# Negated score minima, one probability factor applied on ScalarE, finished heads spilled as one plane

## The chip, the cores and the metric

One NeuronCore of one Trainium2 chip runs the whole kernel. TensorE (PE) does matrix products, VectorE (DVE) and ScalarE (ACT) elementwise work, GpSimd (POOL) a small share of it, and SyncE (SP) issues the DMAs. Each engine takes its instructions in its own fixed order and waits at semaphores for the others. The metric is the device time of one execution in microseconds.

## The reference

A layer of two groups of eight heads over 512 tokens and 16 meta tokens, with one input projection and one output projection:

```python
u = rms_norm(h, g_norm)
rq, rk, rv, rgate, dq, dk, dv, dgate = split(u @ w_in)
r = retention(rq, rk, rv)                     # chunkwise, 8 heads of 128
r = head_layer_norm(r, g_ret) * silu(rgate)
# diff attention, per head, per block of 128 queries:
s = where(allowed, q @ k.T * scale - slope * dist, -inf)     # two maps c = 0, 1
p = softmax(s)
a = p[:, :, 0] - lam * p[:, :, 1]
d = a @ v
d = head_rms_norm(d, g_diff) * (1 - lam_init) * silu(dgate)
y = concatenate([r, d]) @ w_out
out = rms_norm(h + y, final_norm_g)
```

All of it is in float32. The kernel makes each float32 product from parts: an operand is cast to a rounded high part on ScalarE and its low part is a subtraction on VectorE.

## The kernel before

**Stages.** Up to about 130 us the first head is projected; then a loop runs over 29 column pairs of the input projection (rv/rk, rq/rg, dv/dk, dq/dg of the heads in turn), some 98 us for a head of each kind; from about 820 us the output projection runs in five column chunks. Each pair is seven products named P3, P7, P1, P6, P2, P5, P4 of 24 matmuls (`product`, L813, outputs p3, v, x, y). Their weight tiles come by DMA as four raw blocks b11, b12, b21, b22. For each product ScalarE casts the block (wh, L785) and VectorE subtracts (wl, L796); two block sums are made on VectorE (L799, L801), two on GpSimd (L803, L804, each reading two 128x1024 SBUF tiles), L804 after wl_P1 has read b11.

**Order.** `run_pair` issues these products and calls `step()` between them, which moves generators on: `diff_task` (scores, softmax, transposes, the product with the values) and `ret_task`, then `finish` for the head's norm. A scheduler of the tile framework then orders the instructions on every engine with a cost model of its own, so the written order is not what stands on an engine.

**Scores.** In `diff_task` a block b of 128 queries has two maps s. The matmuls L590 (L596 for b = 3) write the scores to one of three PSUM banks shared with other work; L604 on VectorE adds the distance bias, writes p to SBUF, and reduces the maximum mx (the reduction is a second, small instruction). L606 scales mx by -slope; L607 on ScalarE is exp(slope * p + mx) and accumulates the sums zz. L613 and L614 make the two factors rr, L615 scales the second map by rr[1], L616 adds rr[0] times the first. L629 on TensorE transposes the result (at_d), from which L633 and L634 make high and low parts; tile 0 goes through p_std (L438 to L440).

**Finished heads.** `finish` squares and sums a head's output, gets the column sums on TensorE (ms, L463), copies them to SBUF (L464), sends them by DMA to 128 partitions (mc, L467), takes the power on GpSimd (L469 to L472), sends them to DRAM and back as a broadcast (rd, L474; bc, L476, into the sq tile), multiplies (L479, L480), and casts (L485) and subtracts (L486) to the two parts that the output projection reads. Fourteen of the sixteen heads finish before the mix tiles exist; both parts go to DRAM from the r2k buffers (L490) and come back after the loop, straight into the mix tiles, by 28 DMAs of 256 KB. Retention head 7 and diff head 7 finish in output chunk 0, where `mms` runs over pairs of heads and the weight pieces pass through five wr buffers.

## Time and profile before

| | us |
|---|---|
| three runs | 1031.91, 1031.96, 1035.21 |
| median | 1031.96 |
| the profiled execution | 1036.45 |
| its span | 1034.4 |
| TensorE busy in the span | 964.7 |
| VectorE | 824.0 |
| ScalarE | 538.7 |
| GpSimd | 242.7 |

The profiled execution is 4.5 us longer than the median. The span runs from the first to the last recorded instruction. A timeline row is the start, the duration, engine, line, operation, tiles (output <- inputs) and, in brackets, how long the engine had been idle and what it waited for. The recorded durations of consecutive VectorE instructions overlap by about 0.08 us. Tile names in the trace leave out head and block numbers; the order of instructions, shown in the next section, has them.

### The profile page before, as it was taken

Reading aid. Unit: us, or ns where it says so; the run is one execution under the profiler, and the core shown is the slowest. Engines: PE = TensorE matmul, PEld = TensorE weight load, DVE = VectorE, ACT = ScalarE, POOL = GpSimd, SP = SyncE. Lnnn points to the kernel's source line nnn. Section 1 sums busy time; section 2 is a strip of 40 time slices with the busy share of each in tenths; the row PEclk is TensorE's granted clock in tenths of the full one; section 3 lists DMA queues with packets and bytes.
Section 4 is the critical chain, followed back from the end, with each engine's and each line's share of the span. In section 5 each row is a group of like instructions: output and inputs, shape, how many; then the busy total and the mean of one; then the engine's idle time right before and its main releaser. Section 6 shows DMA issues by size and latency. Waiting matters only on the chain.

```text
span 1034.4 us, 18382 instructions
## 1 busy us (share of the span) xinstructions
PE 964.7 (93%) x7215; PEld 921.6 (89%) x7215; DVE 824.0 (80%) x1332; ACT 538.7 (52%) x979; POOL 242.7 (23%) x169
## 2 busy tenths in 40 slices
PE   6999988999999999899999999999994999799997
PEld 6999988999999999899999999999983988588896
DVE  6698869899989998999899989989996754334432
ACT  6454565565656564646565656565654443223322
POOL 4453131132233213321332133233220200000001
PEclk8999999999999999999999999999997999999998
DMA  9512533353235334543643264226443496143304
GB/s 269 158 43 73 125 93 103 82 155 114 82 97 152 107 109 116 139 121 87 140 134 98 82 156 113 83 82 156 113 113 102 161 385 212 50 126 96 122 1 163
DMA packets 166405, 127.03 MB, mean 123 GB/s; under 512 B 9712, under 2 KB 145008, under 8 KB 165808
## 3 DMA queue, kind: packets, MB, share of 16 engines
q1 hardware_dynamic: 165744, 124.04, 42.2%
q10 hardware_dynamic: 576, 1.84, 0.5%
q8 instruction: 56, 0.92, 0.4%
q14 instruction: 29, 0.24, 0.1%
HBM read 107.77 MB, written 11.57 MB: 115 GB/s over the span
## 4 chain that ended last, share of the span: by engine, by line
PE 54%; DVE 21%; DMA 9%; issue 6%; POOL 6%; ACT 4%; SPq 0%; POOLq 0%; DVEq 0%; ACTq 0%
PE y L526 6%; PE y L527 5%; PE y L528 5%; DVE wl_P L796 5%; PE y_rqrg L813 4%; PE x_dvdk L813 3%; PE x_dqdg L813 3%; DMA mc_r<-sq_r 2%; PE x_rqrg L813 2%; PE y_dvdk L813 2%; PE v_rqrg L813 2%; DMA sq_r<-rd_r 2%; PE v_dvdk L813 2%; DVE p_d L615 2%; PE y_rvrk L813 2%
## 5 line engine op out<-in xcount | busy, mean ns | idle before, releaser
L785 ACT CAST wh_P<-b 128x1024 fp32r<-128x1024 f32 x203 | 212.7, 1049 | 147.9 <-DVE mx_d L606 30.3
L796 DVE TENSOR_TENSOR wl_P<-b,wh_P 128x1024 fp32r<-128x1024 f32 x203 | 260.3, 1284 | 13.0 <-ACT wh_P L785 11.0
L803 POOL TENSOR_TENSOR b<-b,b 128x1024 f32<-128x1024 f32 x29 | 69.9, 2412 | 406.1 <-DVE b L799 301.7
L104 DVE TENSOR_TENSOR wl<-wr,wh 128x1024 fp32r<-128x1024 f32 (+1 forms) x40 | 49.8, 1252 | 69.3 <-ACT wh L103 69.2
L804 POOL TENSOR_TENSOR b<-b,b 128x1024 f32<-128x1024 f32 x29 | 76.8, 2649 | 105.5 <-DVE wl_P L796 32.5
L103 ACT CAST wh<-wr 128x1024 fp32r<-128x1024 f32 (+1 forms) x40 | 40.8, 1029 | 88.7 <-PE y L528 70.1
L607 ACT ACTIVATE p_d<-p_d,mx_d 128x144 f32<-128x144 f32 (+3 forms) x64 | 36.6, 572 | 31.7 <-DVE mx_d L606 31.1
L799 DVE TENSOR_TENSOR b<-b,b 128x1024 f32<-128x1024 f32 x29 | 35.5, 1223 | 0.6
L629 PE MATMUL at_d<-ident,p_d 128*128 128x128 f32 (+1 forms) x112 | 23.1, 275 | 13.3 <-DVE p_d L616 12.9
L801 DVE TENSOR_TENSOR b<-b,b 128x1024 f32<-128x1024 f32 x29 | 35.2, 1214 | 0.1
L813 PE MATMUL x_dqdg<-uah,wh_P 128*128 128x256 f32 x128 | 32.2, 290 | 3.0 <-ACT s_dqdg L825 3.0
L1049 POOL TENSOR_SCALAR rs<-ssq,pre 128x1 f32<-128x1 f32 x4 | 1.9, 486 | 136.1 <-ACT jk L1007 136.1
L813 PE MATMUL x_dqdg<-ual,wh_P 128*128 128x256 f32 x128 | 31.2, 282 | 0.0
L526 PE MATMUL y<-wh,mix_s3h 128*128 128x512 f32 (+1 forms) x64 | 23.6, 382 | 6.3 <-ACT mix_s3h L485 5.1
L813 PE MATMUL x_dvdk<-uah,wh_P 128*128 128x264 f32 x112 | 28.5, 284 | 0.0
L813 PE MATMUL x_dvdk<-ual,wh_P 128*128 128x264 f32 x112 | 28.4, 284 | 0.0
L813 PE MATMUL x_rvrk<-uah,wh_P 128*128 128x264 f32 x112 | 28.4, 285 | 0.0
L813 PE MATMUL x_rvrk<-ual,wh_P 128*128 128x264 f32 x112 | 28.2, 285 | 0.0
L629 PEld LDWEIGHTS at_d<-ident,p_d 128*128 128x128 f32 (+1 forms) x112 | 12.8, 126 | 17.3 <-DVE p_d L616 14.8
L813 PEld LDWEIGHTS x_dqdg<-uah,wh_P 128*128 128x128 f32 x128 | 24.1, 188 | 4.2 <-ACT s_dqdg L825 4.2
L526 PE MATMUL y<-wh,mix_s2h 128*128 128x512 f32 (+1 forms) x80 | 27.8, 348 | 0.0
L528 PE MATMUL y<-wh,mix_al 128*128 128x512 f32 (+1 forms) x80 | 27.8, 348 | 0.0
(567 smaller groups left out, 3550.5 us busy)
## 6 DMA issues: line engine op xcount, KB each, us to landing
b<-in_w_in_dram SPq DMA_DIRECT2D x116, 512.0 KB, 4.6
wr<-in_w_out_dram SPq DMA_DIRECT2D x32, 512.0 KB, 4.1
kbuf<-kbuf SPq DMA_DIRECT2D x24, 264.0 KB, 4.9
wr<-in_w_in_dram SPq DMA_DIRECT2D x12, 512.0 KB, 8.5
tab<-in_decay_tab_dram SPq DMA_DIRECT2D x8, 288.0 KB, 4.3
sq_r<-rd_r SPq DMA_DIRECT2D x8, 256.0 KB, 3.6
sq_d<-rd_d SPq DMA_DIRECT2D x8, 256.0 KB, 4.2
mx<-mxh_r SPq DMA_DIRECT2D x7, 256.0 KB, 3.7
```

The costliest lines, as they stand in the source:

```text
L103: act.copy(out=hi, in_=raw)
L104: eng.tensor_tensor(out=lo, in0=raw, in1=f(hi), op=ALU.subtract)
L526: pe.matmul(o, ah, bh, start=start, stop=False)
L527: pe.matmul(o, ah, bl, start=False, stop=False)
L528: pe.matmul(o, al, bh, start=False, stop=stop)
L607: act.activation(p, p, AF.Exp, bias=mx, scale=slope, accum_out=zz[:, s:s + 1])
L629: pe.transpose(at[:n, b * P - q0:(b + 1) * P - q0], aa[b][:, kc:kc + n], ident)
L785: act.copy(out=hi, in_=raw_w[n][SOURCE[pn]])
L796: vec.tensor_tensor(out=lo, in0=w[SOURCE[pn]], in1=f(hi), op=ALU.subtract)
L803: pool.tensor_tensor(out=w["b12"], in0=w["b12"], in1=w["b11"], op=ALU.subtract)
L804: pool.tensor_tensor(out=w["b11"], in0=w["b21"], in1=w["b22"], op=ALU.subtract)
L813: pe.matmul(o, w_[:, kt, :], u[lo][:, kt, c0:], start=not add and w_ is wh and kt == 0 and lo == 0, stop=w_ is wl and kt == 7, skip_group_ ...
```

## The change

Three edits. In the scores the reduction is now a minimum of -slope times the sum (L604's successor L600), so that mx is at once the bias of the exponential, whose scale becomes -1; the 64 L606 go. The second map's factor is applied by ScalarE (L610, an ACTIVATE Copy with a per-partition scale, in place) where VectorE's L615 did it. And a finished head that has no mix tile yet goes to DRAM as it is, from its s2k buffer: 14 writes and 14 reads of 256 KB in place of 28 and 28, no cast and no subtraction in the loop. After the loop `fetch` loads them in pairs into wr buffers and splits each head into its mix tiles with a cast on ScalarE and a subtraction on VectorE, the first two pairs at once, and one more at each step of chunk 0.

```diff
-            hi, lo = heads_mix[col]
+            split(oc, *heads_mix[col])
         else:
-            hi, lo = (ap.tile([P, SEQ], F32R, tag="r2k", bufs=4, name=f"mx{t}_{nm}") for t in "hl")
-        act.copy(out=hi, in_=oc)
-        vec.tensor_tensor(out=lo, in0=oc, in1=f(hi), op=ALU.subtract)
-        if col not in heads_mix:
-            spilled[col] = dr.tile([P, 2, SEQ], F32, tag=f"mx{col}", bufs=1, name=f"mx{col}")
-            for j, t in enumerate((hi, lo)):
-                nc.sync.dma_start(out=spilled[col][:, j, :], in_=f(t))
+            spilled[col] = dr.tile([P, SEQ], F32, tag=f"mx{col}", bufs=1, name=f"mx{col}")
+            nc.sync.dma_start(out=spilled[col], in_=oc)
...
-                vec.tensor_tensor_reduce(shape(p), shape(dist[:, 384 - P * b:]), sp, op0=ALU.add, op1=ALU.max,
-                                         scale=1.0, scalar=-3e38, accum_out=mx)
-                vec.tensor_scalar(mx, mx, -slope, None, op0=ALU.mult)
-                act.activation(p, p, AF.Exp, bias=mx, scale=slope, accum_out=zz[:, s:s + 1])
+                vec.tensor_tensor_reduce(shape(p), shape(dist[:, 384 - P * b:]), sp, op0=ALU.add, op1=ALU.min,
+                                         scale=-slope, scalar=3e38, accum_out=mx)
+                act.activation(p, p, AF.Exp, bias=mx, scale=-1.0, accum_out=zz[:, s:s + 1])
...
-            vec.tensor_scalar(pp[1], pp[1], rr[:, 1:2], None, op0=ALU.mult)
+            act.activation(pp[1], pp[1], AF.Copy, scale=rr[:, 1:2])
...
-    for ks in kpairs:
-        for k in list(range(KT))[ks]:
-            if k in spilled:
-                for j, t in enumerate(heads_mix[k]):
-                    nc.sync.dma_start(out=f(t), in_=spilled[k][:, j, :])
+    fetched = set()
+    def fetch(upto):
+        for i in range(min(upto, len(kpairs))):
+            ks = [k for k in list(range(KT))[kpairs[i]] if k in spilled]
+            if i not in fetched and ks:
+                t = wp.tile([P, 1024], F32, tag="wr", bufs=5, name=f"mb{i}")
+                for j, k in enumerate(ks):
+                    nc.sync.dma_start(out=t[:, j * SEQ:j * SEQ + SEQ], in_=spilled[k])
+                for j, k in enumerate(ks):
+                    split(t[:, j * SEQ:j * SEQ + SEQ], *heads_mix[k])
+            fetched.add(i)
+    fetch(2)
...
+                    fetch(i + 3)
```

Lines below the first edit have lower numbers in the changed file: L604 is L600 there, L613, L614 and L616 are L608, L609 and L611, L518 is L513, L796 is L791, L799 and L801 are L794 and L796, GpSimd's L803 and L804 are L798 and L799, L813 is L808, L829 is L824. Over the whole program VectorE has 1238 instructions for 1334, ScalarE 927 for 895, SyncE 297 for 325, TensorE 7216 in both. TensorE's order is the same up to head 0's scores; from there the scheduler has moved work on all engines. In head 4, whose stretch is 518 to 560 us in the trace, this looks as follows.

VectorE, from the scores of block 0 to block 1's first (p_d4_1_0), before; a name is the tile with head, block and map, wl_17_P6 is the low weight part of pair 17's product P6:

```order
L604 ISA mx_d4_0_1_6540 128x1
L801 TENSOR_TENSOR b22_17_6353<-b22_17_6353,b11_17_6357 128x1024
L606 TENSOR_SCALAR mx_d4_0_0_6532<-mx_d4_0_0_6532 128x1
L693 SCALAR_TENSOR_TENSOR dq4_h_6423<-su2_dqdg4_6393,dq4_h_6423 64x256
L693 SCALAR_TENSOR_TENSOR dq4_l_6424<-su2_dqdg4_6393,dq4_l_6424 64x256
L606 TENSOR_SCALAR mx_d4_0_1_6540<-mx_d4_0_1_6540 128x1
L604 ISA p_d4_1_0_6586,mx_d4_1_0_6587<-dist_617,s_d4_1_0_6583 128x272
```

and now:

```order
L796 TENSOR_TENSOR b22_17_6281<-b22_17_6281,b11_17_6285 128x1024
...
L600 ISA p_d4_0_1_6461,mx_d4_0_1_6462<-dist_617,s_d4_0_1_6458 128x144
...
L513 TENSOR_TENSOR vbuf1_1192<-vp_d4_6439,vbuf1_1192 128x512
L688 SCALAR_TENSOR_TENSOR dq4_h_6351<-su2_dqdg4_6321,dq4_h_6351 64x256
L688 SCALAR_TENSOR_TENSOR dq4_l_6352<-su2_dqdg4_6321,dq4_l_6352 64x256
L791 TENSOR_TENSOR wl_17_P6_6526<-b22_17_6281,wh_17_P6_6524 128x1024
L600 ISA p_d4_1_0_6507,mx_d4_1_0_6508<-dist_617,s_d4_1_0_6504 128x272
```

The block sum of pair 17 (b22) has moved ahead of the scores, and between block 0 and block 1 stand a subtraction of the value split (L513) and one more weight part.

VectorE, at the same head's blocks 2 and 3, before:

```order
L614 TENSOR_TENSOR rr_d4_2_6651<-rr_d4_2_6651,neglam_619 128x1
L796 TENSOR_TENSOR wl_18_P1_6862<-b11_18_6691,wh_18_P1_6860 128x1024
...
L615 TENSOR_SCALAR p_d4_2_1_6646<-p_d4_2_1_6646,rr_d4_2_6651 128x400
L796 TENSOR_TENSOR wl_18_P6_6905<-b22_18_6687,wh_18_P6_6903 128x1024
L616 SCALAR_TENSOR_TENSOR p_d4_2_0_6638<-p_d4_2_0_6638,rr_d4_2_6651,p_d4_2_1_6646 128x400
L604 ISA p_d4_3_1_6742,mx_d4_3_1_6743<-dist_617,s_d4_3_1_6737 128x528
...
L796 TENSOR_TENSOR wl_18_P2_6935<-b21_18_6693,wh_18_P2_6933 128x1024
...
L796 TENSOR_TENSOR wl_18_P5_6985<-b12_18_6689,wh_18_P5_6983 128x1024
...
L615 TENSOR_SCALAR p_d4_3_1_6742<-p_d4_3_1_6742,rr_d4_3_6747 128x528
```

and now:

```order
L611 SCALAR_TENSOR_TENSOR p_d4_2_0_6557<-p_d4_2_0_6557,rr_d4_2_6568,p_d4_2_1_6564 128x400
L794 TENSOR_TENSOR b22_18_6604<-b22_18_6604,b12_18_6606 128x1024
L600 ISA p_d4_3_1_6658,mx_d4_3_1_6659<-dist_617,s_d4_3_1_6653 128x528
...
L791 TENSOR_TENSOR wl_18_P7_6744<-b22_18_6604,wh_18_P7_6742 128x1024
...
L796 TENSOR_TENSOR b22_18_6604<-b22_18_6604,b11_18_6608 128x1024
L609 TENSOR_TENSOR rr_d4_3_6662<-rr_d4_3_6662,neglam_619 128x1
...
L791 TENSOR_TENSOR wl_18_P1_6777<-b11_18_6608,wh_18_P1_6775 128x1024
L791 TENSOR_TENSOR wl_18_P6_6820<-b22_18_6604,wh_18_P6_6818 128x1024
L611 SCALAR_TENSOR_TENSOR p_d4_3_0_6618<-p_d4_3_0_6618,rr_d4_3_6662,p_d4_3_1_6658 128x528
L791 TENSOR_TENSOR wl_18_P2_6850<-b21_18_6610,wh_18_P2_6848 128x1024
```

Block 2's sum (L611, was L616) has moved ahead of P7's and P1's weight parts; block 3's stands behind P6's, where block 2's had stood.

TensorE, at the transposes of the same head in the product x of pair 18, before:

```order
L813 MATMUL x_rqrg5_6932<-ual_123,wh_18_P1_6860 128x256
L813 MATMUL x_rqrg5_6932<-uah_122,wl_18_P1_6862 128x256 x6
L629 MATMUL at_d4_0_6783<-ident_106,p_d4_2_0_6638 16x128
L629 MATMUL at_d4_1_6891<-ident_106,p_d4_2_0_6638 128x128
L813 MATMUL x_rqrg5_6932<-uah_122,wl_18_P1_6862 128x256 x2
```

and now:

```order
L808 MATMUL x_rqrg5_6847<-ual_123,wh_18_P1_6775 128x256
L808 MATMUL x_rqrg5_6847<-uah_122,wl_18_P1_6777 128x256 x3
L624 MATMUL at_d4_0_6698<-ident_106,p_d4_3_0_6618 16x128
L624 MATMUL at_d4_1_6806<-ident_106,p_d4_3_0_6618 128x128
L808 MATMUL x_rqrg5_6847<-uah_122,wl_18_P1_6777 128x256 x5
```

The transposes at this place take block 3 where they took block 2; those of block 2 have gone ahead of it.

ScalarE, at the end of the last diff head (7), where the last norm of the loop (diff head 6) ends, before:

```order
L607 ACTIVATE p_d7_3_0_9812,zz_d7_3_9806<-p_d7_3_0_9812,mx_d7_3_0_9813 128x528
L485 CAST mxh_d6_9906<-oc_d6_9732 128x512
L607 ACTIVATE p_d7_3_1_9863,zz_d7_3_9806<-p_d7_3_1_9863,mx_d7_3_1_9864 128x528
L877 ACT_TABLE_LOAD
L877 ACTIVATE sg_dg7_9564<-sg_dg7_9564 128x512
L825 COPY s37_rvrk7_9644<-p3_rvrk7_9645 128x264
```

and now:

```order
L602 ACTIVATE p_d7_3_1_9735,zz_d7_3_9679<-p_d7_3_1_9735,mx_d7_3_1_9736 128x528
L610 ACTIVATE p_d7_3_1_9735<-p_d7_3_1_9735,rr_d7_3_9739 128x528
L438 CAST p_std_625<-at_d7_0_9779 16x512
L439 CAST p_std_625<-at_d7_0_9779 16x512
L628 CAST ah_d7_1_9892<-at_d7_1_9887 128x512
L872 ACT_TABLE_LOAD
L872 ACTIVATE sg_dg7_9443<-sg_dg7_9443 128x512
L820 COPY s37_rvrk7_9521<-p3_rvrk7_9522 128x264
```

The cast of head 6 is gone; the Copy of block 3, two casts of transposed rows (p_std) and one of the next tile (ah) stand ahead of the table load.

TensorE, in output chunk 0, at the column sums of retention head 7 (ms_r7), whose result that chunk's last piece needs; wh19 is the high part of weight piece 19, before:

```order
L528 MATMUL y0_2_10317<-wh19_10618,mix_al_10283 128x512
L526 MATMUL y0_10314<-wh19_10618,mix_ah_10282 128x512
L527 MATMUL y0_10314<-wl19_10619,mix_ah_10282 128x512
L528 MATMUL y0_10314<-wh19_10618,mix_al_10283 128x512
L463 MATMUL ms_r7_10527<-sh_r7_10506,ones_115 128x512
L526 MATMUL y1_0_10708<-wh20_10648,mix_s4h_10276 128x512
```

and now:

```order
L522 MATMUL y0_10166<-wl18_10476,mix_ah_10148 128x512
L523 MATMUL y0_10166<-wh18_10475,mix_al_10149 128x512
L521 MATMUL y0_0_10167<-wh19_10505,mix_ah_10148 128x512
L463 MATMUL ms_r7_10407<-sh_r7_10379,ones_115 128x512
L522 MATMUL y0_0_10167<-wl19_10506,mix_ah_10148 128x512
L523 MATMUL y0_0_10167<-wh19_10505,mix_al_10149 128x512
```

The sums come before most of piece 19's matmuls, 11 matmuls earlier against the first matmul of retention head 7's own columns, which has kept its place.

## Rows read from the trace of the kernel before

**Rows 1.** The page: the span, and busy us of each engine.
```profile
span 1034.4 us, 18382 instructions
PE 964.7 (93%) x7215; PEld 921.6 (89%) x7215; DVE 824.0 (80%) x1332; ACT 538.7 (52%) x979; POOL 242.7 (23%) x169
```

**Rows 2.** Stretches: length, busy of PE, PEld, DVE, ACT, POOL; PEclk, DMA share, GB/s.
```profile
200.00:750.00 550.00, 530.18 (x4274) 520.61 (x4273) 519.95 (x826) 329.86 (x593) 156.45 (x94) 1.00 0.44 115
767.00:806.00 39.00, 23.18 (x151) 20.92 (x150) 26.46 (x64) 16.53 (x35) 4.24 (x5) 0.78 0.23 68
820.00:880.00 60.00, 60.00 (x337) 52.56 (x337) 32.94 (x51) 23.71 (x41) 4.63 (x5) 1.00 0.85 306
880.00:920.00 40.00, 33.74 (x141) 27.03 (x140) 14.11 (x17) 9.79 (x16) 1.64 (x4) 0.96 0.26 84
```

**Rows 3.** TensorE's waits from 200 to 750: total us, times, longest.
```profile
PE s_d L590 <- DVE mx_d L604: 6.7, 5, 1.4
PE at_d L629 <- DVE p_d L616: 6.7, 5, 2.0
PE x_dqdg L813 <- ACT s_dqdg L825: 3.0, 4, 1.4
```

**Rows 4.** Groups by line and form: total us, mean ns of one | idle before.
```profile
L606 DVE TENSOR_SCALAR mx_d<-mx_d 128x1 f32<-128x1 f32 x64 | 8.3, 147 | 0.2
L615 DVE TENSOR_SCALAR p_d<-p_d,rr_d 128x400 f32<-128x400 f32 x8 | 16.3, 2033 | 0.0
L607 ACT ACTIVATE p_d<-p_d,mx_d 128x400 f32<-128x400 f32 x16 | 10.0, 622 | 3.6 <-DVE mx_d L606 3.6
```

**Rows 5.** Timeline of head 4 around the wait of s_d4_2_1.
```profile
526.99 2.64 POOL L804 TENSOR_TENSOR b<-b,b 128x1024 f32<-128x1024 f32 x1
...
527.40 2.50 DVE L693 SCALAR_TENSOR_TENSOR dq_l<-su_dqdg,dq_l 64x256 fp32r<-64x256 f32 x1
...
530.01 0.43 DVE L604 CUSTOM_DVE_ANT_0 p_d<-dist,s_d 128x272 f32<-128x272 f32 x1
...
530.59 0.60 PE L590 MATMUL s_d<-kbuf,dq_l 128*128 128x400 f32 x2 [1.37 <-DVE mx_d L604]
```

**Rows 6.** Timelines of VectorE, GpSimd and TensorE in head 4, 545 to 558.
```profile
545.32 2.99 DVE L829 TENSOR_TENSOR s_rvrk<-s_rvrk,s_rvrk 128x264 f32<-128x264 f32 x2
...
551.04 1.21 DVE L796 TENSOR_TENSOR wl_P<-b,wh_P 128x1024 fp32r<-128x1024 f32 x1
...
552.87 2.56 DVE L615 TENSOR_SCALAR p_d<-p_d,rr_d 128x400 f32<-128x400 f32 x1
...
545.33 2.69 POOL L803 TENSOR_TENSOR b<-b,b 128x1024 f32<-128x1024 f32 x1 [15.71 <-DVE s_rvrk L829]
552.39 2.81 POOL L804 TENSOR_TENSOR b<-b,b 128x1024 f32<-128x1024 f32 x1 [4.37 <-issue]
...
557.16 0.39 PE L629 MATMUL at_d<-ident,p_d 128*16 128x128 f32 x2 [1.99 <-DVE p_d L616]
```

**Rows 7.** Busy time by stretch behind that wait; PEclk stands third from the end.
```profile
558.00:560.00 2.00, 2.00 (x12) 2.00 (x11) 2.00 (x3) 0.91 (x3) 0.00 (x0) 0.52 0.84 239
560.00:562.00 2.00, 2.00 (x13) 2.00 (x13) 1.68 (x5) 1.22 (x2) 0.00 (x0) 0.63 0.71 204
```

**Rows 8.** Timeline at the last diff head's end.
```profile
788.14 0.43 DVE L615 TENSOR_SCALAR p_d<-p_d,rr_d 128x400 f32<-128x400 f32 x1
...
793.61 0.69 DVE L479 TENSOR_TENSOR oc_d<-oc_d,sq_d 128x512 f32<-128x512 f32 x1 [4.37 <-DMA sq_d<-rd_d]
...
795.62 0.62 ACT L485 CAST mxh_d<-oc_d 128x512 fp32r<-128x512 f32 x1 [7.19 <-DVE oc_d L480]
...
799.23 0.59 PE L813 MATMUL y_rvrk<-s2h,wh_P 128*128 128x264 f32 x1 [9.34 <-ACT s_rvrk L825]
```

**Rows 9.** Timeline in output chunk 0: the column sums, and the wait.
```profile
882.34 0.39 PE L463 MATMUL ms_r<-sh_r,ones 128*128 128x512 f32 x1
...
896.04 0.80 PE L526 MATMUL y<-wh,mix_s3h 128*128 128x512 f32 x1 [5.13 <-ACT mix_s3h L485]
```

## The prediction

> **What bounds the kernel now.** The first view is the page's list of engines: TensorE is busy for 964.7 of 1034.4 us [rows 1], so about 70 us of the span are there to be had, and only where TensorE waits. The table by stretches says where that is: 19.8 us between 200 and 750 (the steady heads), 15.8 between 767 and 806 (the last diff head), none between 820 and 880 and 6.3 between 880 and 920 (the output projection) [rows 2]. In the steady stretch VectorE is busy for 520 of 550 us, ScalarE for 330. The list of waits then names who ends TensorE's waits: in the heads nearly always VectorE, through the score banks (s_d behind L604) and the transposes of the probabilities (at_d behind L616), 6.7 us each in five waits, and ScalarE's s_dqdg with 3.0 us [rows 3]; outside, one wait of 9.3 us and one of 5.1 us, both ended by ScalarE [rows 8, 9]. So the change can pay in three places: five or six like waits per kind in the heads, the gap before the last head's end, and the gap in output chunk 0.
>
> **Work taken off VectorE.** The 64 L606 instructions are 147 ns each, 8.3 us busy, 0.2 idle [rows 4]; less the 0.08 us by which VectorE's records overlap they hold it for 0.07 us each, so some 4 us of VectorE's own time, of which only the part ahead of a waiting TensorE counts. Of the 32 L615 the 128x400 form is 2033 ns on average over eight, 16.3 us [rows 4]. That mean is no work: at 552.87 one lasts 2.56 us because GpSimd's L804 runs from 552.39 to 555.20, and it ends 0.23 us after it [rows 6]. Beside a still GpSimd the same form takes 0.43 us [rows 8]. A removed L615 therefore returns 0.3 to 0.5 us, and the rest only if nothing else on VectorE needs the same access just then. It does: at 545.32 two L829 adds of 264 elements take 2.99 us under L803 [rows 6], and at 527.40 an L693 on 64x256 takes 2.50 us under L804 [rows 5]. Whichever instruction with two SBUF operands stands there, waits GpSimd out.
>
> The Trainium skill ("SBUF — State Buffer", "Who interferes with whom") says the same as a rule: VectorE and GpSimd share one port pair, whoever comes first holds it for the whole instruction, and an instruction with two SBUF inputs counts as one that needs it. By that rule L611 is as exposed as L615 was, and what decides is which of the two stands first at the boundary; the trace agrees for L829 (2.99 us). If VectorE's instruction were always first there, the time would be that of the first rival below.
>
> **What the scaling costs on ScalarE.** The trace of before has no such Copy. The nearest row is the Exp of L607 on the same tile, 622 ns for 400 elements [rows 4]; the Copy saves the accumulator's read and should lie at or below it. Four per head are about 2.2 us of ScalarE, which has 220 us free of 550 [rows 2]: no throughput bound. It adds two handovers, VectorE to ScalarE to VectorE, and behind a waiting Copy stand weight casts (L785) in ScalarE's order. I take 0 for three of the four blocks, since the order puts other VectorE work between L609 and L611, and 0.6 us for block 1, where L611 comes right after L609; the worst would be 0.6 for each.
>
> **The steady heads, one of them walked (head 4, 518 to 560).** Two waits matter.
>
> First, s_d4_2_1. Before, TensorE waits 1.37 us until 530.59, since L693 was held for 2.50 us by GpSimd and p_d4_1_0 comes behind it [rows 5]. Now TensorE has eight more matmuls of 0.12 us ahead of that bank (1.0 us later), but VectorE has the value split's subtraction, L513 on 512 elements (0.6 us, as the 128x512 L479 in [rows 8]) and one more wl (1.21 us, 1.14 to the next start [rows 6]) ahead of p_d4_1_0, less two L606 (0.15). Sum: 0.6 + 1.14 − 0.15 − 1.0 = +0.6; I take +0.5, the GpSimd hold being no longer than before.
>
> Second, at_d4_0, where TensorE waits 1.99 us until 557.16 for block 2's probabilities [rows 6]. By the order, the same place in TensorE's row (3063, now 3064) waits for block 3's. On VectorE block 2 has moved far ahead, no wait there any more; block 3 stands behind wl_P1 and wl_P6. When does it end? Before, wl_P1 starts at 551.04 [rows 6]. Shed ahead of it: two L615 (0.66), L486 (0.6), six L606 (0.4). Added ahead of it: L611 of block 2 and the last L600 (0.54 + 0.63), the shift of the first wait (1.5) and ScalarE's 0.6. That is 551.04 − 1.66 + 3.27 = 552.6. Then wl_P1 and wl_P6 (2 x 1.14) run to 554.9. GpSimd's L804 (L799 in the changed file) is free to start when wl_P1 has been read, waits out wl_P6, and takes the next boundary as at 545.33; 2.81 us later, at 557.7, L611 of 528 elements starts, and ends near 558.4. TensorE comes there at 555.17 + 0.5 − 0.2. So the wait would be about 2.9 us if GpSimd always wins, and 0.2 us if L611 gets in first. The five waits of before had a mean of 1.34 [rows 3]. The rows favour GpSimd (2.99 at 545.32), but the two boundaries are within a microsecond, and the heads differ a little; I take 2.0, so +0.65.
>
> Third, x_dqdg behind s_dqdg, 3.0 us in four waits [rows 3]: VectorE comes out of the head's last block earlier and the mxh casts, which stood in ScalarE's row waiting for a norm's DMA, are gone from it. I take half, −1.5 in all.
>
> Steady heads: 5 x (0.5 + 0.65) − 1.5 = +4.3 us. Bounds: −19.8 (every wait of [rows 2] gone) and +5 x (0.6 + 1.55) = +10.8.
>
> One thing makes long waits dearer: after the 1.99 us wait the granted clock is 0.52 from 558 to 560 and 0.63 from 560 to 562, that is the 1.2 GHz level for a good 3 us, about 1.7 us lost [rows 7]; over the whole stretch it is 1.00 on the mean [rows 2]. Not in the sum, but in the second rival.
>
> **The gap before the last head's end.** TensorE waits 9.34 us until 799.23 [rows 8] behind this chain: the norm's reload ends, L479 at 793.61, L480, the cast mxh_d at 795.62 (0.62), Exp, the table load, Silu, copy of s_rvrk. The cast goes. In its place ScalarE has the Copy of block 3, then two p_std casts and one ah_d cast that wait for TensorE's transposes, then the load and the Silu. From L479 on that is 0.7 + 0.8 (L611) + 0.5 (transposes) + 3 casts (1.7) + the load 1.28 + 0.63 + 0.4 = 6.0 us, against 5.6 before. But the transposes now fall into the gap (1.4 us of TensorE work that used to follow), and ms_d6 stands five TensorE rows earlier, with L450 earlier on VectorE: about 1.5 us. Sum: +0.4 − 1.4 − 1.5 = −2.5. Bounds: 0 and −4.
>
> **The output stage.** Fourteen spills of 256 KB less, each way. Writes are hidden beside the heads: 0. The reloads fall into 820 to 880, where DMA is at 0.85 of its share but TensorE never waits [rows 2]: 0, unless the new splits wait. These are 14 casts and 14 subtractions of 128x512, some 8.7 us of ScalarE and 9.7 of VectorE, in a stretch where these two have 36 and 27 us free. The later gap, 5.13 us until 896.04 [rows 9], starts from ms_r7, issued at 882.34. The same mix_s3h matmul waits, but ms_r7 stands 11 matmuls earlier (y0_0 now comes behind it): 11 x 0.226 (0.39 us each in the record [rows 9], overlapping) = 2.5 us earlier, and the chain behind it is unchanged. So −2.5; bounds 0 (the start of the chain held by ScalarE's casts in front) and −5.1.
>
> **Sum.** +4.3 − 2.5 − 2.5 and about −1.5 for head 0, whose stretch has the same instructions taken out and no walk of mine: −2.2 us. The profiled execution took 1036.45 us (its span 1034.4, 2.05 around it) and would take 1034.2; it lies 4.5 us over the median 1031.96. Put on the median: 1029.8 us. Runs of this kernel can tell apart about 0.3%, 3.1 us.
>
> **Rivals.**
> - VectorE's slack opens: L611 of block 3 gets in ahead of GpSimd in each head, at_d's 6.7 us and s_dqdg's 3.0 vanish, the first wait stays at +0.5 x 5. That is −7.2 in the heads, −6.5 elsewhere: 1018. For it: VectorE is at 520 of 550 us and loses some 4 us a head even where the long forms return only their 0.4. Against it: the order uses the room at once, by putting other work ahead of what TensorE waits for. It decides at one boundary, wl_P6 to L611.
> - The waits grow over 2 us and the clock falls with them (slower). at_d waits 2.9 us in five heads (+7.8), the first wait +2.5, and each time the clock drops once as at 558 (+1.7 x 5, one had it before, so x 4: +6.8). With −1.5 and −6.5: +9, 1041. For it: my own walk ends at 2.9, and the one wait of 1.99 had the drop. Against it: a longer wait also lets VectorE catch up for the next.
> - The splits of chunk 0 are late: ScalarE's casts wait in order for a reload behind weight pieces in the wr buffers, and TensorE, which never waits in 820 to 880, stops for one reload of some 4 us. 1034. Against it: DMA carries 3.7 MB less there.
>
> **How the numbers follow.** The forecast has 0.43, its own range being 1025 to 1035; the first rival 0.27; the second 0.22; the third 0.08. Of the forecast 0.17 lies below 1028.9, 0.23 within 0.3%, 0.03 above. The third is split among the three. So faster 0.45, same 0.27, slower 0.28. The range takes in most of both rivals: 1016 to 1041.
>
> **What would show it.** In the profile after: the 128x400 L615 rows gone, but some L611, wl or L824 rows of 2.3 us and more in their place, starting while GpSimd's L798 or L799 runs; at_d4_0 waiting on L611 of block 3, near 557; the wait before y_rvrk below 9 us with at_d matmuls inside; the wait in chunk 0 near 2.6 us. I would be wrong if GpSimd's instructions mostly met PSUM-reading VectorE work, if TensorE waits within 820 to 880, or if x_dqdg's waits grew because ScalarE is held at a Copy.

## The result and the profile after

The changed kernel takes 1049.28 us (median of 4 runs, 1048.19 to 1051.99) where the kernel before took 1032.77 beside it: a ratio of 1.016, interval 1.0133 to 1.0187. It is slower by 16.5 us; 1029.8 was forecast, with a range up to 1041. The profiled execution took 1049.42 us, its span 1047.6. The profiled execution of before lay 4.5 us over its median, so the two spans differ by 13.2 us only.

First the page's list of engines and its totals, to be read beside [rows 1]:

```profile
span 1047.6 us, 18341 instructions
...
PE 973.2 (93%) x7215; PEld 928.7 (89%) x7215; DVE 813.1 (78%) x1236; ACT 549.7 (52%) x1011; POOL 228.1 (22%) x169
...
HBM read 104.10 MB, written 7.90 MB: 107 GB/s over the span
```

VectorE has lost 10.9 us of busy time, ScalarE has gained 11.0, as meant. The span grew by 13.2 all the same. TensorE, with the same number of matmuls, is busy for 8.5 us more and idle for 4.7 more, so the time is in its clock and in its waits. The table by stretches, for [rows 2] (the columns are the stretch, then the busy time of each engine with its instructions, the granted clock, the DMA share, GB/s):

```profile
200.00:750.00 550.00, 520.98 (x4143) 511.02 (x4142) 490.24 (x723) 322.61 (x588) 136.00 (x91) 0.98 0.40 108
767.00:806.00 39.00, 28.71 (x216) 26.56 (x214) 29.39 (x54) 20.82 (x44) 6.52 (x6) 0.89 0.35 94
820.00:880.00 60.00, 60.00 (x389) 54.87 (x388) 45.40 (x69) 32.07 (x56) 8.01 (x2) 1.00 0.64 231
880.00:920.00 40.00, 34.19 (x142) 26.98 (x142) 17.30 (x23) 12.15 (x20) 3.29 (x8) 0.96 0.34 95
```

In the steady heads TensorE idles 29.0 us where it idled 19.8, and the granted clock is 0.98 where it was 1.00. Between 820 and 880 it is busy throughout in both, so it waits for none of the new splits there. TensorE's waits between 200 and 750, for [rows 3] (total us, times, longest):

```profile
PE y_dqdg L808 <- DVE su_dqdg L824: 18.8, 6, 3.9
PE at_d L624 <- DVE p_d L611: 5.4, 5, 1.1
PE s_d L585 <- DVE dq_h L688: 1.8, 3, 0.8
PE s_d L585 <- DVE rr_d L608: 1.4, 5, 0.3
PE x_dqdg L808 <- ACT s_dqdg L820: 1.1, 2, 0.8
PE s_d L585 <- DVE mx_d L600: 0.3, 2, 0.2
```

In this stretch every kind of wait that the prediction priced has become smaller. The first one is new, 18.8 us in six heads, and the prediction doesn't have it. Its chain, in the timeline around head 3's end and head 4's start (start, duration, engine, line, tiles, and in brackets the idle time before it with what ended it):

```profile
515.30 0.69 DVE L479 TENSOR_TENSOR oc_d<-oc_d,sq_d 128x512 f32<-128x512 f32 x1 [0.65 <-DMA sq_d<-rd_d]
516.02 0.63 ACT L454 ACTIVATE sq_r<-oc_r 64x512 f32<-64x512 f32 x1 [3.86 <-DVE oc_d L479]
516.02 0.75 DVE L480 SCALAR_TENSOR_TENSOR oc_d<-oc_d,gcol,sg_dg 128x512 f32<-128x512 f32 x1
517.63 0.91 SPq L485 DMA_DIRECT2D mx<-oc_d  x1
...
523.20 0.63 ACT L455 ACTIVATE sr_r<-oc_r 64x512 f32<-64x512 f32 x1 [5.34 <-DMA mx<-oc_d]
523.86 0.68 DVE L456 TENSOR_TENSOR sq_r<-sq_r,sr_r 64x512 f32<-64x512 f32 x1 [4.81 <-ACT sr_r L455]
524.47 0.41 DVE L824 TENSOR_TENSOR su_dqdg<-s_dqdg,y_dqdg 128x256 f32<-128x256 f32 x1
...
524.93 0.58 PE L808 MATMUL y_dqdg<-s1h,wh_P 128*128 128x256 f32 x1 [3.91 <-DVE su_dqdg L824]
```

The finished diff head oc_d lies in one of three s2k buffers. The next head's norm needs that buffer for sr_r (L455, on ScalarE). Until the spill has landed in DRAM, L455 waits, 5.34 us; L456 on VectorE, which needs its result, waits 4.81, behind that stands su_dqdg, which needs nothing of either, and TensorE waits 3.91 us for it. Before, the buffer was free as soon as VectorE had read it:

```profile
511.03 0.68 DVE L486 TENSOR_TENSOR mxl_d<-oc_d,mxh_d 128x512 fp32r<-128x512 f32 x1
511.74 0.63 ACT L455 ACTIVATE sr_r<-oc_r 64x512 f32<-64x512 f32 x1 [0.16 <-DVE mxl_d L486]
512.76 0.68 DVE L456 TENSOR_TENSOR sq_r<-sq_r,sr_r 64x512 f32<-64x512 f32 x1
513.37 0.41 DVE L829 TENSOR_TENSOR su_dqdg<-s_dqdg,y_dqdg 128x256 f32<-128x256 f32 x1
```

There the split's two results lay in r2k buffers, and their DMAs held those; this is the cast and the subtraction that the change took out. Over 200 to 820 the L455 wait on the spill is 23.6 us in five heads, longest 5.3, and a sixth head's 4.1 us are put down to "issue"; before, the largest wait of a retention head's L455 for its buffer was 0.2.

The clock comes on top. Stretches of 2 us behind that wait in the changed kernel (the granted clock is third from the right):

```profile
522.00:524.00 2.00, 0.00 (x0) 0.00 (x0) 0.14 (x1) 0.78 (x2) 0.00 (x0) 1.00 1.15 313
524.00:526.00 2.00, 1.07 (x5) 1.07 (x6) 1.95 (x3) 2.00 (x3) 0.00 (x0) 0.61 0.73 181
526.00:528.00 2.00, 2.00 (x12) 2.00 (x12) 1.94 (x3) 0.64 (x2) 0.00 (x0) 0.53 0.18 50
528.00:530.00 2.00, 2.00 (x18) 1.95 (x17) 1.91 (x4) 1.03 (x3) 0.00 (x0) 1.00 0.75 220
```

After a wait of 3.91 us TensorE runs at its 1.2 GHz level for some 3 us. If each 2 us stretch below 0.95 counts with what it lacks to 1.00, the clock takes 8.5 us between 200 and 750, behind four of the six waits; the other two, of 2.5 us each (until 624.45 and 723.91), have no slow stretch behind them. Before it took 1.7, in one head [rows 7]. The two windows from 200 to 750 don't hold the same work. From head 1's first score matmul to head 6's they do; before, then now:

```profile
228.90:718.43 489.53, 472.36 (x3798) 463.32 (x3796) 461.00 (x731) 294.28 (x526) 136.38 (x81) 1.00 0.43 114
228.66:730.52 501.86, 476.67 (x3798) 467.65 (x3796) 448.60 (x661) 295.29 (x535) 121.75 (x80) 0.99 0.39 106
```

The same 3798 matmuls take 12.3 us longer: 8.0 us more idle (25.2 for 17.2) and 4.3 us more busy, at a granted clock of 0.99 for 1.00. By the starts, head 1's first score matmul stands at 228.66 for 228.90 (−0.2), head 6's at 730.52 for 718.43 (+12.1), y_rvrk of the last pair at 813.55 for 799.23 (+14.3), the span's end +13.2.

### The profile page after: what moved, and what is told of

Same layout as the page of the kernel before. It is cut to its first block, busy times and chain, and to the rows that moved or that the text cites. A ratio compares the mean times of both kernels' runs of the same rounds, so it can differ in the third digit from the quotient of the medians.

```text
span 1047.6 us, 18341 instructions
## 1 busy us (share of the span) xinstructions
PE 973.2 (93%) x7215; PEld 928.7 (89%) x7215; DVE 813.1 (78%) x1236; ACT 549.7 (52%) x1011; POOL 228.1 (22%) x169
## 4 chain that ended last, share of the span: by engine, by line
PE 51%; DVE 26%; DMA 8%; ACT 7%; issue 6%; POOL 2%; SPq 0%; POOLq 0%; DVEq 0%; ACTq 0%
DVE wl_P L791 8%; PE y L521 5%; PE y L523 5%; PE y L522 5%; PE y_rqrg L808 3%; PE y_dvdk L808 3%; PE x_dvdk L808 3%; DVE p_d L611 3%; DMA mx<-oc_d 3%; PE x_rqrg L808 2%; DMA sq_d<-rd_d 2%; PE v_rqrg L808 2%; ACT wh_P L780 2%; PE y_dqdg L808 2%; DVE s_dvdk L824 2%
## 5 line engine op out<-in xcount | busy, mean ns | idle before, releaser
L791 DVE TENSOR_TENSOR wl_P<-b,wh_P 128x1024 fp32r<-128x1024 f32 x203 | 270.4, 1337 | 20.1 <-ACT wh_P L780 13.9
L798 POOL TENSOR_TENSOR b<-b,b 128x1024 f32<-128x1024 f32 x29 | 71.5, 2464 | 318.9 <-DVE b L794 303.2
L799 POOL TENSOR_TENSOR b<-b,b 128x1024 f32<-128x1024 f32 x29 | 80.6, 2780 | 135.5 <-DVE wl_P L791 61.7
L602 ACT ACTIVATE p_d<-p_d,mx_d 128x144 f32<-128x144 f32 (+3 forms) x64 | 36.6, 572 | 25.2 <-DVE mx_d L600 25.1
L624 PE MATMUL at_d<-ident,p_d 128*128 128x128 f32 (+1 forms) x112 | 23.7, 282 | 18.3 <-DVE p_d L611 17.8
L808 PE MATMUL y_dqdg<-s1h,wh_P 128*128 128x256 f32 x64 | 21.5, 355 | 18.8 <-DVE su_dqdg L824 18.8
L611 DVE SCALAR_TENSOR_TENSOR p_d<-p_d,rr_d,p_d 128x144 f32<-128x144 f32 (+3 forms) x32 | 32.9, 1030 | 6.6 <-ACT p_d L610 6.6
L794 DVE TENSOR_TENSOR b<-b,b 128x1024 f32<-128x1024 f32 x29 | 35.4, 1220 | 0.3
L796 DVE TENSOR_TENSOR b<-b,b 128x1024 f32<-128x1024 f32 x29 | 35.3, 1216 | 0.1
L808 PEld LDWEIGHTS y_dqdg<-s1h,wh_P 128*128 128x128 f32 x64 | 16.0, 250 | 20.1 <-DVE su_dqdg L824 20.1
L808 PE MATMUL x_dqdg<-uah,wh_P 128*128 128x256 f32 x128 | 31.7, 286 | 1.1 <-ACT s_dqdg L820 1.1
L624 PEld LDWEIGHTS at_d<-ident,p_d 128*128 128x128 f32 (+1 forms) x112 | 12.8, 128 | 22.1 <-DVE p_d L611 20.1
L808 PE MATMUL x_dqdg<-ual,wh_P 128*128 128x256 f32 x128 | 31.0, 281 | 0.0
L808 PE MATMUL x_rqrg<-uah,wh_P 128*128 128x256 f32 x112 | 28.1, 286 | 0.7 <-DVE vT_rvrk L824 0.7
L808 PE MATMUL x_rvrk<-uah,wh_P 128*128 128x264 f32 x112 | 28.6, 287 | 0.0
L808 PE MATMUL x_rvrk<-ual,wh_P 128*128 128x264 f32 x112 | 28.1, 284 | 0.0
L808 PE MATMUL x_dvdk<-uah,wh_P 128*128 128x264 f32 x112 | 28.1, 285 | 0.0
```

Source lines behind the costliest of these rows:

```text
L602: act.activation(p, p, AF.Exp, bias=mx, scale=-1.0, accum_out=zz[:, s:s + 1])
L611: vec.scalar_tensor_tensor(pp[0], pp[0], rr[:, 0:1], pp[1], op0=ALU.mult, op1=ALU.add)
L791: vec.tensor_tensor(out=lo, in0=w[SOURCE[pn]], in1=f(hi), op=ALU.subtract)
L798: pool.tensor_tensor(out=w["b12"], in0=w["b12"], in1=w["b11"], op=ALU.subtract)
L799: pool.tensor_tensor(out=w["b11"], in0=w["b21"], in1=w["b22"], op=ALU.subtract)
L808: pe.matmul(o, w_[:, kt, :], u[lo][:, kt, c0:], start=not add and w_ is wh and kt == 0 and lo == 0, stop=w_ is wl and kt == 7, skip_group_ ...
```

## The experiments

The first theory was the held buffer, all of the loss by the chain above; its rival, that the edits of the scores make an order in which TensorE waits. A second theory, on L479's place, came up on the way. The order here is the sequence of instructions that the scheduler puts on each engine. Nearly every edit changed it on all engines, far from the edited lines too, so a difference between two kernels holds the edit and the new order together. In two pairs it stayed: on VectorE and GpSimd from the changed kernel to e17, and on all four engines from e24 to e26. All ratios are to the kernel before, run on the same chip; its medians there were 1035.3 to 1035.7 us. "Clock lost" is counted between 200 and 750 as above.

| run | what it is | ratio (95% interval) | TensorE's largest kind of wait, 200 to 750 | clock lost, us |
|---|---|---|---|---|
| e5_min_only | edit 1, minimum | 1.0029 (1.0009 to 1.0049) | at_d 7.2 | 1.7 |
| e6_scale_only | edit 2, scaling on ScalarE | 0.9954 (0.9932 to 0.9976) | at_d 4.4 | 0 |
| e2_scores_only | edits 1 and 2 | 1.0073 (1.0047 to 1.0098) | at_d 9.5 | 3.4 |
| e3_spill_only | edit 3, spill | 1.0223 (1.0191 to 1.0255) | dq_h 23.7 | 10.3 |
| e25_after_old_max | edits 2 and 3 | 1.0110 (1.009 to 1.013) | y_dqdg 15.1 | 8.5 |
| e17_spill_twice | all, two DMAs per spill | 1.0174 (1.0131 to 1.0217) | v_dqdg 22.4 | 15.2 |
| e4_spill_from_r2k | all, spill from r2k | 1.0048 (1.0031 to 1.0064) | dq_h 16.9 | 10.2 |
| e14_norm_on_gpsimd | as e4, norm's end on GpSimd | 1.0194 (1.0139 to 1.0249) | x_dqdg 21.6 | 11.9 |
| e8_r2k_spill_only | edit 3 from r2k | 1.0121 (1.0084 to 1.0159) | dq_h 18.9 | 6.8 |
| e27_scale_r2k | edit 2, and 3 from r2k | 1.0061 (1.004 to 1.0083) | dq_h 18.0 | 10.2 |
| e20_r2k_gated | as e8, L479 held back | 1.0058 (1.0036 to 1.008) | s_d on mx_d 10.1 | 10.2 |
| e24_scale_r2k_gated | as e27, L479 held back | 0.9944 (0.9923 to 0.9964) | x_dqdg 5.2 | 0 |
| e21_after_r2k_gated | as e4, L479 held back | 1.0071 (1.0044 to 1.0099) | s_d on rr_d 12.8 | 12.0 |
| e26_min_kept_slot | as e21, 64 small instructions kept | **0.9920 (0.9896 to 0.9945)** | at_d 4.4 | 0 |
| e22_before_gated | before, L479 held back | 1.0041 (1.0024 to 1.0058) | s_r 6.1 | 0 |

**Which edit costs.** Two runs at first: the two edits of the scores with the old spill (the spill and the reload as in the kernel before), and the spill edit with the old scores.

> The two edits of the scores, with the spill of before (two planes from the r2k buffers). Theory, the held buffer: a finished head's s2k buffer is now busy until its spill has landed, ScalarE's L455 waits for it in order, and TensorE waits before the second half of y_dqdg. Then this kernel has no wait of y_dqdg at su_dqdg over 0.5 us and takes 1020 to 1033 us. Rival, the handover: the Copy on ScalarE between two VectorE instructions has shifted the order and made the waits; then the six waits of y_dqdg of 2.5 to 3.9 us are here too, and it takes 1043 to 1050 us.

> The scores of before, and only the spill of one plane from the s2k buffer. The held buffer: ScalarE's L455 waits for the spill's landing, five or more times, 20 us or more in all, TensorE's y_dqdg waits 15 us or more in all, and it takes 1042 to 1052 us. The handover: nothing of that, 1026 to 1034 us.

The spill alone is slower than the whole change (1058.49 us, above both ranges), but not in the way that the theory told. L455 waits 20.3 us in six heads for its DMA, as it said; yet VectorE waits only 3.3 us behind it, and TensorE has no wait for su_dqdg. Its waits stand at dq_h, 23.7 us in five, a place to which a later part comes back; in head 4 dq_h stands behind the retention head's L479 and lasts 2.52 us itself, beside GpSimd's L799. So the spill does harm in this order, but that the held buffer does it here isn't shown. The edits of the scores were not the gain they were expected to be, 1.0073, a time in the rival's range without the rival's waits: no y_dqdg wait, but at_d 9.5 us in five, and 13.1 us in four between 750 and 820, where it had been 4.6 in three. Each of them alone:

```diff
-                                         scale=1.0, scalar=-3e38, accum_out=mx)
-                vec.tensor_scalar(mx, mx, -slope, None, op0=ALU.mult)
+                                         scale=-slope, scalar=3e38, accum_out=mx)
```

> Only the reduction to an already scaled minimum, 64 small VectorE instructions fewer. Held buffer and handover alike: no cause of the loss is in it, 1026 to 1032 us; the 2.0 to 2.6 us forms of L615 stay. If any move of the order costs, it is slower than before by some us.

```diff
-            vec.tensor_scalar(pp[1], pp[1], rr[:, 1:2], None, op0=ALU.mult)
+            act.activation(pp[1], pp[1], AF.Copy, scale=rr[:, 1:2])
```

> Only the Copy on ScalarE in place of L615. The spill is that of before. Both scores' edits together gave 1.0073, the minimum alone 1.0029. The handover theory in its weak form: this edit carries the rest, 1.003 to 1.007, with VectorE waiting at L616 for ScalarE some 6 us in all. The order theory: any value from 0.995 to 1.008, and where it is above 1.0 the waits stand behind another instruction than L616.

The kernel with the scaling alone is faster: waits between 200 and 750 down to 4.4 for at_d, no stretch at the lower clock. The one with the minimum alone is a little slower (1026 to 1032 us were expected, it took 1039.35), and adding the minimum to the scaling costs 1.2 per cent (0.9954 to 1.0073). Whether the edits or their orders do this stayed open until the last runs.

**The held buffer.** Its test is to let the spill leave from another buffer, with the scores as changed:

```diff
-        vec.scalar_tensor_tensor(oc, oc, gcol[:, col:col + 1], T[gate], op0=ALU.mult, op1=ALU.mult)
+        on = oc if col in heads_mix else ap.tile([P, SEQ], F32, tag="r2k", bufs=4, name=f"on_{nm}")
+        vec.scalar_tensor_tensor(on, oc, gcol[:, col:col + 1], T[gate], op0=ALU.mult, op1=ALU.mult)
...
-            nc.sync.dma_start(out=spilled[col], in_=oc)
+            nc.sync.dma_start(out=spilled[col], in_=on)
```

> The changed kernel, but the last multiplication of a spilled head (L480) writes into an r2k buffer, from which the spill then goes, so that its s2k buffer is free at once. No instruction more or less. The held buffer: L455 waits for no DMA, y_dqdg's 18.8 us of waits and the low clock behind them (some 6 us) go, and it takes 1021 to 1031 us. The handover: 1043 to 1050 us, since the Copy is still there. A third possibility, that any move of the order costs: between 1032 and 1043.

L455 waits for no DMA any more, the y_dqdg waits are gone, and 1.016 becomes 1.0048. But 1040.15 us lies in the third possibility's range and not in the held buffer's: the order has changed, and TensorE now waits 16.9 us for dq_h. The writes also land sooner. The last number of these rows is the median of issue to landing between 200 and 750, in us, in the changed kernel and then here:

```profile
mx<-oc_d SPq DMA_DIRECT2D x6, 256.0 KB, 5.3
mx<-on_d SPq DMA_DIRECT2D x6, 256.0 KB, 2.0
```

In e3, from the s2k buffer, it is 2.0 too, so the same 256 KB hold their buffer for very different times; what makes the difference isn't shown. The other direction, a spill that holds the buffer longer (the head is written to a second DRAM tile too, with VectorE's order the same):

```diff
             nc.sync.dma_start(out=spilled[col], in_=oc)
+            nc.sync.dma_start(out=again, in_=oc)
```

> The changed kernel, with each spill written a second time from the same s2k buffer, to a DRAM tile that nothing reads. VectorE's order is the same instruction for instruction, TensorE's work too; only the buffer is busy for one more DMA of 256 KB (2 to 5 us). The held buffer: ScalarE's wait of L455 for the spill grows from 23.6 us in five by 1.5 to 3 us each, the waits of y_dqdg from 18.8 by 8 to 18, and with the clock behind them the time is 8 to 25 us above the changed kernel's, at a ratio of 1.024 to 1.04 to the kernel before. If the held buffer isn't what TensorE waits for (the rivals: the handover to ScalarE, or the order), the time stays within 3 us of the changed kernel's (1.013 to 1.019).

The size missed: the second DMA lands right behind the first and adds only 0.6 us to a wait, and the ratio lies within the interval of the whole change; the profiled span is 1047.6 in both. The waits did follow the hold: L455 has 31.3 us in six heads against 27.7 in six (one of them counted as issue), 3.6 more, and TensorE has 22.4 for 18.8, again 3.6 more (now at v_dqdg, whose weight cast stands behind L455 on ScalarE). The clock lost is 15.2 us for 8.5. From head 1's first score to head 6's this kernel takes 505.1 us for 501.9; behind that the difference is gone again. So this run bears out the path from the buffer to TensorE, and its dose was too small to show in the whole time. The next test is the change without its minimum:

> The changed kernel with the old maximum: scaling on ScalarE and the one-plane spill from the s2k buffer. Held-buffer theory: ScalarE's L455 waits for the spill's DMA for 20 us or more in the heads, TensorE has waits of 3 us and more behind it and low-clock stretches; ratio 1.008 to 1.025. Rival (it was mostly the order that the minimum makes, and the buffer's wait is covered in another order): L455 waits but TensorE doesn't, 0.995 to 1.004.

Two rows of its waits, TensorE's and ScalarE's:

```profile
PE y_dqdg L808 <- DVE su_dqdg L824: 15.1, 5, 3.5
...
ACT sr_r L455 <- DMA mx<-oc_d: 23.6, 6, 4.9
```

The same pair of waits; with the spill from r2k (e27, below) these edits have neither, and with L479 in place as well they give 0.9944. So the held buffer makes the y_dqdg waits without the minimum too. By e3, where the same wait of L455 was covered, its harm depends on what stands behind L455 in the order. A fourth s2k buffer, the plainest test, wasn't tried.

**The second loss: L479 comes too early.** With the spill from r2k there was still a wait that before doesn't have, TensorE's s_d on dq_h, and it shows with the old scores too:

> The scores of before; only the spill of one plane, but written to an r2k buffer by L480 and sent from there. Against the spill from s2k alone (ratio 1.022). The held buffer: L455 waits for no DMA, and the ratio is 0.995 to 1.006. A second theory, formed on the runs so far: whatever shifts VectorE's order puts a multiplication L479, which waits for the norm's DMA, ahead of work that TensorE needs; then VectorE is idle at L479 for 15 us or more in the heads, TensorE waits for dq_h, and the ratio is 1.004 to 1.015.

L455 waits for no DMA, and still 1.0121 lies in the second theory's range, with 34.2 us of waits at L479. The timeline of the run with scaling and r2k spill (e27) has the chain in four rows:

```profile
531.92 0.69 DVE L479 TENSOR_TENSOR oc_r<-oc_r,sq_r 128x512 f32<-128x512 f32 x1 [6.09 <-DMA sq_r<-rd_r]
532.76 0.69 DVE L514 TENSOR_TENSOR vbuf<-vp_d,vbuf 128x512 fp32r<-128x512 f32 x1
533.47 0.42 DVE L689 SCALAR_TENSOR_TENSOR dq_h<-su_dqdg,dq_h 64x256 fp32r<-64x256 f32 x1
...
533.95 0.63 PE L586 MATMUL s_d<-kbuf,dq_h 128*128 128x400 f32 x2 [3.56 <-DVE dq_h L689]
```

The retention head's L479 waits 6.09 us for its factors, which come by three DMAs and GpSimd's power, and dq_h stands behind it on VectorE. Before, L479 stood behind block 1's probabilities, after the DMA. The scheduler has moved it up; what made it do so isn't shown. One attempt took the norm's two multiplications to GpSimd and the gain factor to ScalarE:

> The changed kernel with the spill from r2k, and for the fourteen spilled heads the two multiplications behind the norm's DMA on GpSimd in place of VectorE (two products of 512 elements, the column's factor in a ScalarE Copy into r2k). So no VectorE instruction of a spilled head waits for a DMA. If such waits in VectorE's order cost the time: the waits of TensorE for dq_h (16.9 us with r2k alone) go, and the ratio is 0.985 to 0.998. If not, or if GpSimd's own order (its block sums behind these products) takes their place: 1.0 to 1.015.

The wait moved on instead, and 1.0194 lies above both ranges: ScalarE's L454 now waits 24.2 us for GpSimd, and TensorE 21.6 us for ScalarE's s_dqdg behind it. An in-order engine that takes on an operand from a DMA chain passes the wait to whatever stands behind. The other attempt holds L479 at its old place, by letting it read a 128x1 tile of ones made from block 1's first probabilities:

```diff
-        vec.tensor_tensor(out=oc, in0=oc, in1=bc, op=ALU.mult)
+            vec.tensor_scalar(one, state.pop("gate"), 0.0, 1.0, op0=ALU.mult, op1=ALU.add)
+            vec.scalar_tensor_tensor(oc, oc, one, bc, op0=ALU.mult, op1=ALU.mult)
```

> Old scores, one-plane spill from an r2k buffer as in the run of the spill edit alone from r2k (1.0121), and one thing more: the retention head's L479 is made to stand behind block 1's probabilities in VectorE's order, where it stood before the change, by reading a 128x1 tile that is made from them. Order theory (the loss left after the r2k buffer comes from L479 standing ahead of dq_h L689 while its factors' DMA is still under way): TensorE's waits on dq_h, 18.9 us in 6 (max 4.4), fall under 5 us, L479's waits on the DMA from 34.2 us to under 10, ratio 0.995 to 1.004. Rival (the shorter tail of the head's norm shifts all other work and TensorE waits elsewhere): the dq_h waits go, but at_d or s_d waits of 2 us and more take their place and the ratio stays above 1.008.

> The scaling on ScalarE (0.9954 alone) with the one-plane spill from an r2k buffer and L479 held behind block 1's probabilities; the old maximum. Order theory: what the scaling gives stays and the spill costs nothing, ratio 0.990 to 0.998. Rival (each edit shifts the scheduler's order anew, so gains don't add): 1.000 to 1.010, with a wait of 2 us and more in each head at a place that neither part alone has.

> As the run that gave 0.9944 (scaling on ScalarE, spill from r2k, old maximum), without the gate on the retention head's L479. Order theory: L479 stands ahead of dq_h again and waits there for its factors' DMA, dq_h waits of 10 us and more in all, ratio 1.003 to 1.010. Rival (the gain is the scaling's, the gate is idle): 0.992 to 0.998, dq_h waits under 5 us.

The last two differ in one edit, the gate: dq_h waits of 18.0 us and 1.0061 without it, none and 0.9944 with it. That L479's place makes the dq_h waits is shown; the 1.2 points hold also what else moved in the order. With the old scores the gate removes the dq_h waits too (18.9 to 0.8), but 10.1 us of s_d waits come up and only half of the loss goes; that was the rival's expectation in kind, but 1.0058 lies between the two ranges. The control says how much of such differences is mere order:

> Control: the kernel before with only the same reading of a 128x1 tile by the retention head's L479, which stands behind block 1's probabilities there anyway. Order theory: nothing moves that TensorE waits for, ratio 0.997 to 1.003. Rival (the added small instruction, or the later L479, has a price of its own): above 1.003, with L479's successors, the casts of the two parts, waited for.

One small instruction per head, with L479 where it had been, costs 0.4 per cent (at most 0.3 were expected), the waits now at s_r (6.1 us) and dq_h (3.6). Between orders, differences of this size are no evidence on an edit; that goes for the two single edits of the scores above, too.

**The minimum.** With the buffer free and L479 held, the changed scores still lost:

> The changed kernel with the spill from an r2k buffer (1.0048) and the retention head's L479 held behind block 1's probabilities in VectorE's order. Order theory: the dq_h waits, 16.9 us in 6, fall under 5 us, ratio 0.99 to 1.002. Rival (the new minimum costs by itself, 1.0029 alone): TensorE waits on rr_d and at_d as in the run of the minimum alone, ratio 1.002 to 1.008.

The time is the rival's, with 12.8 us of waits in six heads at the same bank; its reason is tested below. The timeline of this run:

```profile
532.65 2.42 POOL L811 TENSOR_TENSOR b<-b,b 128x1024 f32<-128x1024 f32 x1
532.88 2.47 DVE L700 SCALAR_TENSOR_TENSOR dq_l<-su_dqdg,dq_l 64x256 fp32r<-64x256 f32 x1
...
535.47 0.42 DVE L610 CUSTOM_DVE_ANT_0 p_d<-dist,s_d 128x272 f32<-128x272 f32 x1
...
536.04 0.95 PE L595 MATMUL s_d<-kbuf,dq_l 128*128 128x400 f32 x2 [2.13 <-DVE rr_d L621]
```

GpSimd's block sum starts 0.23 us ahead of dq_l, which reads two SBUF tiles and lasts 2.47 us (0.42 in e27, with GpSimd still); the bank's reader L610 stands behind it, and TensorE's 2.13 us are followed by the lower clock (12.0 us over the stretch). The Trainium skill ("SBUF — State Buffer", "Who interferes with whom") has it that a VectorE instruction with two SBUF inputs contends with a GpSimd instruction that reads SBUF, and that the order of issue decides who blocks; the trace agrees, dq_l ending 0.28 us after GpSimd's block sum, as at 527.40 in [rows 5]. Is this the minimum's doing, or the order's? The next run keeps the 64 small instructions, as multiplications by 1.0, so that all four engines have instruction for instruction the order of e24:

```diff
+                vec.tensor_scalar(mx, mx, 1.0, None, op0=ALU.mult)
                 act.activation(p, p, AF.Exp, bias=mx, scale=-1.0, accum_out=zz[:, s:s + 1])
```

> The changed kernel with the spill from r2k and L479 held, as in the run that gave 1.0071, but the 128x1 multiplication of the minimum stays in VectorE's order, by 1.0. That puts every instruction of TensorE and VectorE in the same order as in the run with the old maximum that gave 0.9944. Theory (the new minimum costs nothing itself; without the 64 small instructions the scheduler makes another order, in which GpSimd's block sum meets dq_l L700 just ahead of a score bank, and TensorE's clock falls): 0.991 to 0.998, no granted clock below 0.95 between 200 and 750, s_d waits under 5 us. Rival (the reduction with a scale and a minimum is slower, or the Exp with scale -1 waits for it): 1.004 to 1.010, with s_d waits of 2 us each as in the run without the multiplication.

The waits of this run, and its steady stretch in the table by stretches:

```profile
PE at_d L637 <- DVE p_d L624: 4.4, 6, 1.0
PE x_dqdg L821 <- ACT s_dqdg L833: 4.2, 7, 0.7
PE x_rqrg L821 <- ACT s_rqrg L833: 2.6, 5, 0.5
PE s_d L595 <- ACT p_d L613: 1.9, 2, 1.0
```

```profile
200.00:750.00 550.00, 536.26 (x4318) 524.62 (x4318) 516.02 (x806) 332.85 (x608) 156.27 (x94) 1.00 0.42 111
```

0.9920, TensorE 536.3 us busy of 550 at full clock: nearly the same waits as e24, and the lowest ratio of the study (1027.79 us beside 1035.32), though not clear of e24's. The new minimum costs nothing itself. What cost 1.3 points from e24 to e21 was that 64 instructions of 0.07 us had gone and the scheduler had put the rest otherwise. That the 1.2 points from e6 to e2 are of the same kind is likely by this, and wasn't tried.

## Why the prediction was wrong

**The failed step** is one clause in the output stage: "Writes are hidden beside the heads: 0". It counted the bytes of the spills and asked whether TensorE waits for DMA; it didn't ask which buffer the write keeps, and who needs that buffer next. The trace of before had the rows for it: ScalarE's L455 came 0.03 us after L486 had read the buffer (511.74, above), so a longer hold was on L455 at once, and writes of 256 KB (mxh_d) took 4.2 us from issue to landing at the median. In the changed kernel the write took 5.5 us (517.63 to about 523.1), and L455 waited 5.34 us, TensorE 3.91. The third rival looked at the reloads, in 820 to 880, where nothing happened. The forecast would not have come true with this term put right, either: with the spill from r2k the ratio is 1.0048 (e4), where the forecast was 0.998. The rest is the order, above all L479's place, which the walk took from the kernel before.

The other terms, as forecast and as measured in the changed kernel. Single kinds of wait are those between 200 and 750, and parts of the heads' row; the rows of stretches (head 0, heads 1 to 5, the last head's end, the output stage) add up to the span's +13.2:

| term | predicted, us | measured, us |
|---|---|---|
| s_d, five heads | +2.5 | 6.7 and 1.0 on dq_h became 3.5 in all: −4.2 |
| at_d, five heads | +3.25 | 6.7 became 5.4: −1.3 |
| x_dqdg | −1.5 | 3.0 became 1.1: −1.9 |
| writes, the held buffer | 0 | +18.8 of waits in six heads; clock lost 8.5 for 1.7 |
| heads 1 to 5 in all | +4.3 | +12.3 |
| gap before the last head's end | −2.5 | +14.3 less +12.1: +2.2 for the stretch; TensorE's idle time in it 17.7 for 18.5: −0.8 |
| output stage | −2.5 | +13.2 less +14.3: −1.1 |
| head 0 | −1.5 | head 1's first score at 228.66, for 228.90: −0.2, with the first y_dqdg wait (2.59) in it |

- **The heads.** The small waits fell where the forecast had two of the three kinds grow. TensorE's new stop of 2 to 4 us in each head may have let VectorE catch up; that isn't shown, and e6, e24 and e26, which have no such stop, have at_d at 4.4. That x_dqdg came near its term is no proof of it, since it is 1.8 in e6 and 5.2 in e24. The mechanism named for at_d is there: L615's rows are gone, and L611 of 528 elements now takes 2359 ns on the mean of eight, 766 for its counterpart before. In head 4, one lasts 2.90 us from 563.73, under GpSimd's L799 (562.80, 3.26 us). The time that L615 gave back was taken by the next instruction with two SBUF operands, as the prediction said.
- **The Copy on ScalarE** was sized rightly: 629 ns for 400 elements, where 622 was to be the bound, and VectorE idles 4.6 us in eight heads ahead of block 1's sum, 0.6 each, as forecast.
- **The last head's gap** was to lose the cast's time. L479 there waits 4.86 us for the norm's DMA, and L611 of block 3 stands behind it (808.28), so that at_d waits 7.81 us until 809.10, and the wait of y_rvrk is 0.24. So the transposes did fall into the gap, but the gap as a whole lost 0.8 us and not 2.5, and the granted clock between the two starts was 0.90 for 0.92. It is the second loss of the experiments in another place: work that TensorE needs stands behind L479, whose row the walk took as given.
- **The output stage** went as told but smaller, a wait of 3.9 for 5.13; TensorE has no wait in 820 to 880.
- **The rivals.** The second had the right multiplier, the clock, though not behind each wait (four of six). It put this at at_d and reached 1041; the wait that did it was one that the text doesn't name. The first, VectorE's slack, has its condition met in e24 and e26: the sum of 528 elements takes 763 and 762 ns there, so GpSimd doesn't hold it up. They give 0.9944 and 0.9920; the latter is 7.5 us, where the rival gave 13.7 (1031.96 to 1018), and at_d and s_dqdg keep 4.4 and 4.2 us of the waits that were to vanish.
- **What was to show it wrong** (PSUM-reading work under GpSimd, waits in 820 to 880, a Copy that holds ScalarE up): none of these happened. The list covered the terms of the sum and not the one that had been set to zero.

How the 16.5 us divide among the edits can't be told exactly, since each kernel gets its own order. By the runs that differ in one edit, each with its new order: the held buffer 1.1 points (1.016 to 1.0048) and the minimum 0.5 (1.016 to 1.0110); L479's place and the slots of the minimum together 1.3 (1.0048 to 0.9920). These are no parts of one sum, and the control's 0.4 and the 1.5 points that order alone made (e21 to e26) say how loosely they are to be read. The waits that came and went with each edit stand firmer than the points.
